# Softmax divided on GpSimd, in place on the probabilities, instead of on the gate

## The chip, the cores and the metric

The kernel runs on one core of a Trainium2 chip. The metric is the device time of one execution in microseconds (us). The core has five engines that run side by side, each through its own instructions in a fixed order: PE (TensorE, the matrix engine; its weight loads are listed apart as PEld), DVE (VectorE), ACT (ScalarE), POOL (GpSimd) and SP (SyncE, which here issues the DMA transfers). An instruction that needs another engine's result waits on a semaphore, and everything behind it on its own engine waits with it.

## The reference

One encoder layer is applied to two sequences of 2048 tokens with 1024 channels. After an RMS norm and one input projection, two attention branches run with 8 heads of 64 channels each: branch A attends inside a window of +-128 tokens and has 2 key heads and a learned sink, branch B attends to a neighbourhood of 8 x 16 on a grid of 64 columns with a learned bias. Each branch output is multiplied by SiLU of its gate, and output projections follow. What matters here:

```
# branch A, per block of 128 queries        # branch B, per grid row
m = max(max(sc), sink)                      pr = softmax(sc)
e = exp(sc - m)                             o  = pr @ v
denom = sum(e) + exp(sink - m)              o_b = o * silu(g_b)
pr = e / denom
o  = pr @ v
o_a = o * silu(g_a)
```

Division by the denominator is one factor per query and head, so it may be applied to the probabilities before the product with V, or to the gate that multiplies the product.

## The kernel before

The work is cut into 96 tiles of 128 tokens: `f` 0 to 31 is branch A (both sequences), 32 to 95 branch B in two halves of the heads. While tile `f` has its attention, PE fills the gaps with projection matmuls of later tiles (`stream`, made of `filler(f)`). Two tables, `PLAN_A` and `PLAN_B`, say at which share of a tile's projection work each piece of attention is emitted. PE's instructions are chained in exactly the order in which they are written (`pinned`); the instructions of ACT, DVE, POOL and SP are placed by a list scheduler that sees the dependencies.

An attention unit is four heads of one tile: branch A has two units for each `f` (`kv` 0 and 1), 64 in all, branch B one for each `f`, 64 in all. A unit goes through these steps:

- `sc(i)`, i = 0 to 3: two score matmuls for head i into a bank of PSUM; `softmax` then lets DVE add the mask or bias, write the scores to the SBUF tile `s` and take their row maximum.
- Behind `sc(3)`, `exps`: DVE negates the maxima (`nm`), ACT takes four exponentials in place on the four `s` tiles with their sums into `den`, branch A adds the sink, and DVE takes the reciprocal `rd`. DVE then multiplies `rd` by the token's norm factor `fct` (a column of `y` or `hr_b`), and POOL multiplies the 256 gate columns of the unit by it into a new tile `g2` (shown as `g` in the profile).
- `pt(j)`: PE transposes the probabilities into PSUM. In branch A, `pt(0)` transposes the first 128 columns of all four heads, `pt(1)` the next; in branch B, `pt(x)` transposes one head, in the order of heads 0, 2, 1, 3. ACT copies each result to SBUF as its high part and DVE makes the low part.
- `po`: PE multiplies the transposed probabilities with V.
- `fin` (in the next unit's time): PE transposes `g2`, and DVE multiplies it with the output.

A score row has 384 columns in branch A (256 at the ends of a sequence), and 288, 360, 384 or 512 in branch B. The gate `gs` of a tile lies in one of 6 buffers tagged `qg`, which also hold the queries.

The waits that matter are in these places: `pt` reads `s`, so it waits for whoever wrote `s` last; POOL also makes the low parts of the projections' inputs (L279), the rotary embedding of branch A (L405 to L408), the sum of two output halves in branch B (L694) and weight sums (L461).

Of the kernel before, what the change touches and what calls it, by code (L numbers as in the profile page):

```python
# [11 lines left out]
F32 = mybir.dt.float32  # L12
# [3 lines left out]
ALU = mybir.AluOpType  # L16
# [6 lines left out]
HD = 64  # L23
# [61 lines left out]
def emit(ctx, tc, io):  # L85
    nc = tc.nc
# [4 lines left out]
    def ptile(shape, tag, name):  # L91
        tag = PSM.get(tag, tag)
        return pp.tile(shape, F32, tag=tag, name=name, bufs=PSB[tag])
# [100 lines left out]
    def project(ps, xr, w, cost):  # L194

        for k in range(KT):
            for i, (a, b) in enumerate(((0, 0), (0, 1), (1, 0))):
                mm(ps, xr[:, a, k, :], w(k, b), k == 0 and i == 0, k == KT - 1 and i == 2)
                yield cost, k == KT - 1 and i == 2
# [11 lines left out]
    def exps(sm, n, fct, gs, sink=None):  # L211

        mx, nm, den, rd, ss = (sm[k] for k in ("mx", "nm", "den", "rd", "s"))
        if sink is None:
            nc.vector.tensor_scalar_mul(nm, mx, -1.0)  # L215
        else:
            nc.vector.scalar_tensor_tensor(out=nm, in0=mx, scalar=-1.0, in1=sink[1], op0=ALU.mult, op1=ALU.min)
        for i in range(4):
            nc.scalar.activation(ss[i][:, :n], ss[i][:, :n], AF.Exp, bias=nm[:, i:i + 1],  # L219
                                 accum_out=den[:, i:i + 1])  # L220
        if sink is not None:
            es = ap.tile([128, 4], F32, tag="es", name="es", bufs=3)
            nc.vector.tensor_tensor(out=es, in0=sink[0], in1=nm, op=ALU.add)
            nc.scalar.activation(es, es, AF.Exp)
            nc.vector.tensor_tensor(out=den, in0=den, in1=es, op=ALU.add)
        nc.vector.reciprocal(out=rd, in_=den)
        nc.vector.tensor_scalar_mul(rd, rd, fct)  # L227
        g2 = ap.tile([128, 4, HD], F32, tag="g2", name="g2", bufs=2)
        nc.gpsimd.tensor_tensor(out=g2, in0=gs.rearrange("p (h d) -> p h d", h=4),  # L229
                                in1=rd.unsqueeze(2).broadcast_to([128, 4, HD]), op=ALU.mult)  # L230
        return g2.rearrange("p h d -> p (h d)")

    def split_q(pqt, q1, q2):

# [10 lines left out]
    ap = ab_stack.enter_context(tc.tile_pool(name="ab", bufs=1))  # L245
# [98 lines left out]
    for i in range(4):  # L344
        nc.vector.tensor_tensor(out=tab[i // 2][:, i % 2], in0=cs[:, i % 2],
                                in1=rw[:, i].unsqueeze(1).broadcast_to([128, NT, 16]), op=ALU.mult)
# [29 lines left out]
    def proj_a(f):  # L376
        s, t = divmod(f, NT)
        xr, ms, (ssq, ee) = xt.pop(f), ms_a[:, f:f + 1], stats.pop(f)
        ka = 22 if f in last else KA
        pk = ptile([128, 256], "pj", "pk")  # L380
        yield from project(pk, xr, lambda k, b: wx[:, k, b, :], 112)
        sq2 = ap.tile([128, 512], F32, tag="sq", name="sq2", bufs=2)
        nc.scalar.activation(sq2[:, :128], pk[:, 0:128], AF.Square)
        nc.vector.tensor_reduce(out=ssq[:, 8:10], in_=sq2[:, :128].rearrange("p (h d) -> p h d", d=HD),
                                op=ALU.add, axis=AX.X)
        vr = ap.tile([128, 11], F32, tag="vr", name="vr", bufs=2)
        y = ap.tile([128, 12], F32, tag="y", name="y", bufs=4)
        nc.vector.tensor_scalar(out=vr[:, 8:10], in0=ssq[:, 8:10], scalar1=1.0 / HD, scalar2=ee,
                                op0=ALU.mult, op1=ALU.add)
        nc.vector.tensor_scalar(out=vr[:, 10:11], in0=ms, scalar1=EPS, scalar2=None, op0=ALU.add)  # L390
        rsqrt(ap, vr[:, 8:11], y[:, 8:11], 3, "rqk")
        nc.vector.tensor_scalar_mul(y[:, 11:12], y[:, 10:11], 0.5)
        kt = ap.tile([128, 4, HD], F32, tag="kt", name="kt", bufs=2)
        nc.vector.tensor_tensor(out=kt[:, 0:2, :], in0=pk[:, 0:128].rearrange("p (h d) -> p h d", d=HD),
                                in1=y[:, 8:10].unsqueeze(2).broadcast_to([128, 2, HD]), op=ALU.mult)
        pv = pk[:, 128:256].rearrange("p (h d) -> p h d", d=HD)
        nc.scalar.activation(vv[:, t, :, 0, :], pv, AF.Copy, scale=y[:, 10:11])
        nc.vector.scalar_tensor_tensor(out=vv[:, t, :, 1, :], in0=pv, scalar=y[:, 10:11],
                                       in1=vv[:, t, :, 0, :].bitcast(F32), op0=ALU.mult, op1=ALU.subtract)

        def rope(v, n, tb):
            r = ap.tile([128, 2, 8, 16], F32, tag="vr_", name="r", bufs=2)
            cb_ = tab[tb][:, 0, t, :].unsqueeze(1).broadcast_to([128, n, 16])
            sb_ = tab[tb][:, 1, t, :].unsqueeze(1).broadcast_to([128, n, 16])
            nc.gpsimd.tensor_tensor(out=r[:, 0, :n], in0=v[:, :, 0:16], in1=cb_, op=ALU.mult)  # L405
            nc.gpsimd.tensor_tensor(out=r[:, 1, :n, 0:8], in0=v[:, :, 8:16], in1=sb_[:, :, 0:8], op=ALU.mult)
            nc.gpsimd.tensor_tensor(out=r[:, 1, :n, 8:16], in0=v[:, :, 0:8], in1=sb_[:, :, 8:16], op=ALU.mult)
            nc.gpsimd.tensor_tensor(out=v[:, :, 0:16], in0=r[:, 0, :n], in1=r[:, 1, :n], op=ALU.add)  # L408
        rope(kt[:, 0:2, :], 2, 1)
        yield 0, False  # L410
        pq = ptile([128, 512], "pj", "pq")
        for i, c in enumerate(project(pq, xr, lambda k, b: w_q[k][:, b, :], 215)):
            if i in HQ and f > 0:
                HQ[i][0](f + 1, HQ[i][1])
            if i - 10 in HG and f in last:
                HG[i - 10][0](f + 1, HG[i - 10][1])
            yield c
            if i == ka:
                keys_a(kt, t)
        sq = ap.tile([128, 512], F32, tag="sq", name="sq", bufs=2)  # L420
        nc.scalar.activation(sq, pq, AF.Square)
        nc.vector.tensor_reduce(out=ssq[:, 0:8], in_=sq.rearrange("p (h d) -> p h d", d=HD), op=ALU.add, axis=AX.X)
        nc.vector.tensor_scalar(out=vr[:, 0:8], in0=ssq[:, 0:8], scalar1=1.0 / HD, scalar2=ee,
                                op0=ALU.mult, op1=ALU.add)
        rsqrt(ap, vr[:, 0:8], y[:, 0:8], 8, "rqa")
        q = ap.tile([128, 8, HD], F32, tag="qg", name="q", bufs=6)
        nc.vector.tensor_tensor(out=q, in0=pq.rearrange("p (h d) -> p h d", d=HD),
                                in1=y[:, 0:8].unsqueeze(2).broadcast_to([128, 8, HD]), op=ALU.mult)
        rope(q, 8, 0)
        yield 0, False  # L430
        pg = ptile([128, 512], "pj", "pg")
        for i, c in enumerate(project(pg, xr, lambda k, b: w_g[k][:, b, :], 215)):
            if i in HG and f > 0 and f not in last:
                HG[i][0](f + 1, HG[i][1])
            yield c
            if i + 24 == ka:
                keys_a(kt, t)
        gs = ap.tile([128, 512], F32, tag="qg", name="gs", bufs=6)
        nc.scalar.activation(gs, pg, AF.Tanh, scale=y[:, 11:12])
        nc.vector.scalar_tensor_tensor(out=gs, in0=gs, scalar=1.0, in1=pg, op0=ALU.add, op1=ALU.mult)  # L440
        held[f] = q, gs, y
        if t == NT - 1:
            regroup(s)
        if f == NT + 4:
            stats_b(0)
        yield 0, False
# [22 lines left out]
    def regroup(s):  # L469
        c = slice(NT * s, NT * s + NT)  # L470
        nc.sync.dma_start(ms_d[s * SEQ:(s + 1) * SEQ].rearrange("(t p) -> p t", p=128), ms_a[:, c])
        rows = ms_d.rearrange("(r k c) -> r k c", k=4, c=16)
        for i in range(NT * s, NT * s + NT):
            nc.sync.dma_start(ms_b[:, i:i + 1], rows[8 * (i // 4):8 * (i // 4) + 8, i % 4, :].rearrange("r c -> c r"))
# [84 lines left out]
    def proj_b(f):  # L559
# [11 lines left out]
        for i, c in enumerate(project(pk, xr, lambda k, b: w_qk[k][:, b, :], 215)):  # L571
            at = i + 24 if f in last else i
            if at in HX:
# [8 lines left out]
        nc.vector.tensor_scalar(out=vr, in0=ssq, scalar1=1.0 / HD, scalar2=ep_b[:, st:st + 1],  # L582
                                op0=ALU.mult, op1=ALU.add)
        rsqrt(ap, vr, y, 8, "rqb")
        qg = ap.tile([128, 2, 4, HD], F32, tag="qg", name="qg", bufs=6)
        kt = ap.tile([128, 4, HD], F32, tag="kt", name="kb", bufs=2)
        for dst, c in ((kt, 4), (qg[:, 0], 0)):
            nc.vector.tensor_tensor(out=dst, in0=pk[:, 64 * c:64 * c + 256].rearrange("p (h d) -> p h d", d=HD),
                                    in1=y[:, c:c + 4].unsqueeze(2).broadcast_to([128, 4, HD]), op=ALU.mult)
# [3 lines left out]
        for i, c in enumerate(project(pv, xr, lambda k, b: w_vg[k][:, b, :], 215)):  # L593
# [3 lines left out]
            if i == (KB if f not in last else 10):  # L597
                if f < 2 * NT + 2:
                    pending.append((kt, b, cb))
                else:  # L600
# [5 lines left out]
                                       in1=v[:, :, 0, :].bitcast(F32), op0=ALU.mult, op1=ALU.subtract)  # L606
# [5 lines left out]
        gs = qg[:, 1].rearrange("p h d -> p (h d)")  # L612
# [251 lines left out]
    with tc.tile_pool(name="c", bufs=1) as op:  # L864
# [179 lines left out]
        for m in range(7 * len(groups)):  # L1044
            n, i = divmod(m, 7)
# [104 lines left out]
```

## Time and profile before

| | before |
|---|---|
| median of 3 runs | 2651.11 us (2646.79 to 2652.35) |
| span of the profiled execution | 2651.7 us |
| the profiled execution's own time | given as its span alone; nothing is listed around it |
| granted TensorE clock over the span | 0.990 |
| PE busy | 2570.5 us, 97% |
| PE weight loads | 2270.6 us, 86% |
| DVE busy | 1952.0 us, 74% |
| ACT busy | 1500.2 us, 57% |
| POOL busy | 703.2 us, 27% |

The span lies within the three runs, 0.6 us over their median, so sums made against it hold for the runs too. Branch A's units run from about 60 to 830 us, branch B's from about 890 to 1940 us, and the rest is the output projection. A busy time of PE says that matmuls follow one another, not that each is as fast as it can be, so the idle time and the granted clock have to be read with it.

### The profile page before, as it was taken

Reading aid. Unit: us, or ns where it says so; the run is one execution under the profiler, and the core shown is the slowest. Engines: PE = TensorE matmul, PEld = TensorE weight load, DVE = VectorE, ACT = ScalarE, POOL = GpSimd, SP = SyncE. Lnnn points to the kernel's source line nnn. Section 1 sums busy time; section 2 is a strip of 40 time slices with the busy share of each in tenths; the row PEclk is TensorE's granted clock in tenths of the full one; section 3 lists DMA queues with packets and bytes.
Section 4 is the critical chain, followed back from the end, with each engine's and each line's share of the span. In section 5 each row is a group of like instructions: output and inputs, shape, how many; then the busy total and the mean of one; then the engine's idle time right before and its main releaser. Section 6 shows DMA issues by size and latency. Waiting matters only on the chain. (4 is left out here: it accounts for less than half of the span.)

```text
span 2651.7 us, 46657 instructions
## 1 busy us (share of the span) xinstructions
PE 2570.5 (97%) x16080; PEld 2270.6 (86%) x16080; DVE 1952.0 (74%) x5702; ACT 1500.2 (57%) x3519; POOL 703.2 (27%) x804
## 2 busy tenths in 40 slices
PE   7999999999989999999899999999989999999999
PEld 6888878888877888888788888888989999999999
DVE  6888878888887788788888888788665548555554
ACT  5776667676765566666676666666532214222322
POOL 3222222222222223223223222221123323223321
PEclk9999999999999999999999999999999999999999
DMA  6333322111233455555655554446675445223221
GB/s 208 101 100 102 108 74 77 58 55 52 55 98 117 150 170 171 181 177 160 221 167 165 185 170 153 148 152 205 184 235 195 158 158 194 79 97 107 80 76 48
DMA packets 230973, 357.48 MB, mean 135 GB/s; under 512 B 38321, under 2 KB 115761, under 8 KB 225585
## 3 DMA queue, kind: packets, MB, share of 16 engines
q1 hardware_dynamic: 230736, 354.51, 42.4%
q8 instruction: 127, 2.08, 0.3%
q14 instruction: 110, 0.89, 0.1%
HBM read 266.33 MB, written 105.92 MB: 140 GB/s over the span
## 5 line engine op out<-in xcount | busy, mean ns | idle before, releaser
L219 ACT ACTIVATE s<-s,nm 128x384 f32<-128x384 f32 (+4 forms) x512 | 306.3, 600 | 274.9 <-DVE nm L215 183.7
L189 PE MATMUL pvg<-wb,xr 128*128 128x512 f32 x1536 | 457.4, 405 | 0.0
L189 PE MATMUL pqk<-wa,xr 128*128 128x512 f32 x1536 | 436.6, 407 | 0.0
L279 POOL TENSOR_TENSOR xr<-stx,xr 128x512 fp32r<-128x512 f32 x192 | 246.9, 1296 | 396.1 <-ACT xr L278 369.2
L189 PEld LDWEIGHTS pqk<-wa,xr 128*128 128x128 f32 x1536 | 267.1, 189 | 36.8
L189 PEld LDWEIGHTS pvg<-wb,xr 128*128 128x128 f32 x1536 | 269.1, 190 | 31.8
L189 PE MATMUL pg<-wb,xr 128*128 128x512 f32 x768 | 231.9, 409 | 1.3 <-ACT wb L142 0.9
L189 PE MATMUL pq<-wa,xr 128*128 128x512 f32 x768 | 223.0, 404 | 3.5 <-DVE wa L143 2.3
L973 PE MATMUL acca<-opd,s 128*128 128x256 f32 x1344 | 169.6, 289 | 15.2 <-DVE r L992 13.6
L973 PEld LDWEIGHTS acca<-opd,s 128*128 128x128 f32 x1344 | 167.7, 197 | 15.8 <-DVE r L992 10.0
L189 PEld LDWEIGHTS pq<-wa,xr 128*128 128x128 f32 x768 | 141.6, 191 | 27.3 <-DVE wa L143 2.6
L204 DVE CUSTOM_DVE_ANT_0 s<-scb,bias 128x288 f32<-128x288 f32 (+3 forms) x256 | 141.9, 555 | 30.3 <-PE scb L189 26.4
L229 POOL TENSOR_TENSOR g<-qg,rd 128x256 f32<-128x256 f32 x64 | 39.2, 613 | 453.4 <-DVE rd L227 385.8
L668 DVE TENSOR_TENSOR p_t<-ptb,p_t 96x384 fp32r<-96x384 f32 (+3 forms) x256 | 149.6, 586 | 12.6 <-ACT p_t L667 9.1
L189 PEld LDWEIGHTS pob<-p_t,vw 128*128 128x128 f32 (+2 forms) x832 | 130.7, 190 | 32.4 <-ACT q1b L240 15.5
L189 PEld LDWEIGHTS pg<-wb,xr 128*128 128x128 f32 x768 | 137.2, 189 | 22.5 <-DVE wb L143 1.4
L667 ACT CAST p_t<-ptb 96x384 fp32r<-96x384 f32 (+3 forms) x256 | 129.8, 509 | 46.8 <-PE ptb L192 44.8
L556 DVE SCALAR_TENSOR_TENSOR ks_b<-pktb,wk,ks_b 64x128 fp32r<-64x128 f32 x256 | 115.2, 450 | 53.9 <-ACT ks_b L555 47.3
L189 PE MATMUL pob<-p_t,vw 128*128 128x256 f32 (+2 forms) x832 | 143.2, 285 | 5.4 <-ACT q1b L240 5.4
L189 PE MATMUL sc<-ks_a,q 128*128 128x384 f32 (+1 forms) x512 | 133.0, 351 | 13.2 <-DVE mx L204 6.4
L555 ACT ACTIVATE ks_b<-pktb,wk 64x128 fp32r<-64x128 f32 x256 | 124.9, 489 | 20.2 <-DVE ks_b L556 12.2
L204 DVE CUSTOM_DVE_ANT_0 s<-sc,mask 128x384 f32<-128x384 f32 (+1 forms) x256 | 136.0, 533 | 0.2
(197 smaller groups left out, 5826.3 us busy)
## 6 DMA issues: line engine op xcount, KB each, us to landing
stx<-x_b SPq DMA_DIRECT2D x128, 256.0 KB
vw<-v_d SPq DMA_DIRECT2D x112, 256.0 KB
stx<-x_a SPq DMA_DIRECT2D x64, 256.0 KB
stn<-x_n SPq DMA_DIRECT2D x64, 256.0 KB
v_d<-vb SPq DMA_DIRECT2D x64, 256.0 KB
x1r<-x_d SPq DMA_DIRECT2D x16, 1024.0 KB
y_t<-r SPq DMA_DIRECT2D x64, 256.0 KB
v_d<-vb SPq DMA_DIRECT2D x96, 128.0 KB
```

The lines of the kernel that those rows point to most:

```text
L189: pinned(nc.tensor.matmul(out, lhsT, rhs, start=start, stop=stop))
L204: nc.vector.tensor_tensor_reduce(out=s[:, :n], in0=ps[:, :n], in1=bias, scale=1.0, scalar=-3.0e38, op0=ALU.add, op1=ALU.max, accum_out=sm[ ...
L219: nc.scalar.activation(ss[i][:, :n], ss[i][:, :n], AF.Exp, bias=nm[:, i:i + 1], accum_out=den[:, i:i + 1])
L229: nc.gpsimd.tensor_tensor(out=g2, in0=gs.rearrange("p (h d) -> p h d", h=4), in1=rd.unsqueeze(2).broadcast_to([128, 4, HD]), op=ALU.mult)
L279: nc.gpsimd.tensor_tensor(out=lo, in0=raw, in1=hi.bitcast(F32), op=ALU.subtract)
L555: nc.scalar.activation(hi, pkt[a:a + 64, i], AF.Copy, scale=wk[a:a + 64, 1:2])
L556: nc.vector.scalar_tensor_tensor(out=lo, in0=pkt[a:a + 64, i], scalar=wk[a:a + 64, 1:2], in1=hi.bitcast(F32), op0=ALU.mult, op1=ALU.subtract)
L667: nc.scalar.copy(p_t[:kc, :nch, 0], pf)
L668: nc.vector.tensor_tensor(out=p_t[:kc, :nch, 1], in0=pf, in1=p_t[:kc, :nch, 0].bitcast(F32), op=ALU.subtract)
L973: pinned(nc.tensor.matmul(ps[:, kk], w[k][:, a, c:c + 128], o[:, b, k], start=i in (0, 1, 4) and kk == 0 and k == 0 and j == 0, stop=k == ...
```

## The change

The gate is left as it is. DVE's multiplication of `rd` by `fct` goes, and so does POOL's multiplication of the gate. Instead POOL multiplies each of the four `s` tiles, in place, by its head's column of `rd` and by `fct`: four instructions for a unit, each over all columns of the score row. The transposes of the gate in `fin` read `gs` directly. Since `gs` is now needed until `fin`, tag `qg` gets 7 buffers instead of 6; the two buffers of `g2` are gone.

```diff
@@ exps
         nc.vector.reciprocal(out=rd, in_=den)
-        nc.vector.tensor_scalar_mul(rd, rd, fct)
-        g2 = ap.tile([128, 4, HD], F32, tag="g2", name="g2", bufs=2)
-        nc.gpsimd.tensor_tensor(out=g2, in0=gs.rearrange("p (h d) -> p h d", h=4),
-                                in1=rd.unsqueeze(2).broadcast_to([128, 4, HD]), op=ALU.mult)
-        return g2.rearrange("p h d -> p (h d)")
+        for i in range(4):
+            nc.gpsimd.tensor_scalar(out=ss[i][:, :n], in0=ss[i][:, :n], scalar1=rd[:, i:i + 1], scalar2=fct,
+                                    op0=ALU.mult, op1=ALU.mult)
+        return gs
@@ proj_a (q and gs) and proj_b (qg)
-        q = ap.tile([128, 8, HD], F32, tag="qg", name="q", bufs=6)
+        q = ap.tile([128, 8, HD], F32, tag="qg", name="q", bufs=7)
...
```

In the listings below a row is a line of the kernel, an operation, what it writes and reads, and the tile's size; x4 is a run of four alike. Lines of the changed kernel are numbered one lower from L230 on.

POOL's order in branch A before, over one unit with `kv` 0 and one with `kv` 1:

```order
L405 TENSOR_TENSOR r<-kt,tab_203 128x32
L406 TENSOR_TENSOR r<-kt,tab_203 128x2x8
L407 TENSOR_TENSOR r<-kt,tab_203 128x2x8
L408 TENSOR_TENSOR kt<-r 128x2x16
L229 TENSOR_TENSOR g_3284<-gs,rd 128x256
L405 TENSOR_TENSOR r<-q,tab_202 128x128
L406 TENSOR_TENSOR r<-q,tab_202 128x8x8
L407 TENSOR_TENSOR r<-q,tab_202 128x8x8
L408 TENSOR_TENSOR q<-r 128x8x16
L229 TENSOR_TENSOR g_3439<-gs,rd 128x256
L279 TENSOR_TENSOR xr<-stx,xr 128x512 x2
```

The same place now:

```order
L404 TENSOR_TENSOR r<-kt,tab_203 128x32
L405 TENSOR_TENSOR r<-kt,tab_203 128x2x8
L406 TENSOR_TENSOR r<-kt,tab_203 128x2x8
L407 TENSOR_TENSOR kt<-r 128x2x16
L228 TENSOR_SCALAR s<-s,rd,y 128x384 x4
L404 TENSOR_TENSOR r<-q,tab_202 128x128
L405 TENSOR_TENSOR r<-q,tab_202 128x8x8
L406 TENSOR_TENSOR r<-q,tab_202 128x8x8
L407 TENSOR_TENSOR q<-r 128x8x16
L228 TENSOR_SCALAR s<-s,rd,y 128x384 x4
L278 TENSOR_TENSOR xr<-stx,xr 128x512 x2
```

The four instructions stand exactly where the one stood; nothing else on POOL changes its place in branch A.

PE's order is the same row by row, but for the gate's name in `fin`. One unit of branch A with `kv` 0, before; the three rows of `pt` are those that read `s`:

```order
L192 MATMUL pgt<-ident,g_3439 128x128 x2
L189 MATMUL pq<-wa_99,xr 128x512
L189 MATMUL pq<-wa_100,xr 128x512 x3
L189 MATMUL pq<-wa_101,xr 128x512 x3
L189 MATMUL pq<-wa_102,xr 128x512 x2
L192 MATMUL pt<-ident,s 128x128 x4
L189 MATMUL pq<-wa_102,xr 128x512
L192 MATMUL pt<-ident,s 128x128 x4
L189 MATMUL pg<-wb_103,xr 128x512 x3
L192 MATMUL pt<-ident,s 128x128 x4
L189 MATMUL pg<-wb_104,xr 128x512 x3
```

No projection matmul has been moved between the scores and the transposes.

ACT's order around the transposes of a unit with `kv` 1, before and then now (`pr` is the copy of a transpose's result, `xr` the high part of a later tile's input):

```order
L537 COPY ot<-po 64x256
L278 CAST xr<-stx 128x512
L240 CAST q_3473<-pqt 64x512
L237 CAST q_3474<-pqt 64x512
L517 CAST pr<-pt 128x512 x2
L240 CAST q_3474<-pqt 64x512
L517 CAST pr<-pt 128x512
L278 CAST xr<-stx 128x512
```

```order
L536 COPY ot<-po 64x256
L239 CAST q_3491<-pqt 64x512
L236 CAST q_3492<-pqt 64x512
L516 CAST pr<-pt 128x512
L277 CAST xr<-stx 128x512
L516 CAST pr<-pt 128x512
L239 CAST q_3492<-pqt 64x512
L516 CAST pr<-pt 128x512
L277 CAST xr<-stx 128x512
```

The first `xr` now stands behind the first copy of a transpose instead of ahead of it. DVE and SP have a few such swaps of neighbours; on DVE the multiplication of `rd` (L227) is gone.

More of the change, by code (lines that the diff above doesn't have):

```diff
@@ L437, in proj_a @@
                 keys_a(kt, t)
-        gs = ap.tile([128, 512], F32, tag="qg", name="gs", bufs=6)
+        gs = ap.tile([128, 512], F32, tag="qg", name="gs", bufs=7)
         nc.scalar.activation(gs, pg, AF.Tanh, scale=y[:, 11:12])
@@ L584, in proj_b @@
         rsqrt(ap, vr, y, 8, "rqb")
-        qg = ap.tile([128, 2, 4, HD], F32, tag="qg", name="qg", bufs=6)
+        qg = ap.tile([128, 2, 4, HD], F32, tag="qg", name="qg", bufs=7)
         kt = ap.tile([128, 4, HD], F32, tag="kt", name="kb", bufs=2)
```

## The prediction

> **What bounds the kernel now.** I read the page's busy times first, then the list of PE's waits, then the timeline of single units in branch A and branch B.
>
> ```profile
> span 2651.7 us, 46657 instructions
> PE 2570.5 (97%) x16080; PEld 2270.6 (86%) x16080; DVE 1952.0 (74%) x5702; ACT 1500.2 (57%) x3519; POOL 703.2 (27%) x804
> PE pt L192 <- ACT s L219: 6.3, 4, 5.3
> ```
>
> PE is idle for 2651.7 - 2570.5 = 81 us in all, and of the probabilities' transposes `pt` only four had to wait for the exponentials, 6.3 us together. No row of PE's waits names POOL. So PE sets the time, its order is fixed, and each microsecond that an instruction of PE waits is a microsecond of the end unless PE would have waited later anyway. The question is how close behind the softmax the transposes stand. A unit of branch A with `kv` 0, then one with `kv` 1 (start, length, engine, line, operation):
>
> ```profile
> 250.90 0.61 ACT L219 ACTIVATE s<-s,nm 128x384 f32<-128x384 f32 x1
> 251.50 0.19 ACT L224 ACTIVATE es<-es 128x4 f32<-128x4 f32 x1
> 251.99 0.18 DVE L226 RECIPROCAL rd<-den 128x4 f32<-128x4 f32 x1
> 252.46 0.21 DVE L227 TENSOR_SCALAR rd<-rd,y 128x4 f32<-128x4 f32 x1
> 252.60 0.58 PEld L192 LDWEIGHTS pt<-ident,s 128*128 128x128 f32 x4
> 252.75 0.61 POOL L229 TENSOR_TENSOR g<-gs,rd 128x256 f32<-128x256 f32 x1 [1.13 <-DVE rd L227]
> 252.83 0.60 PE L192 MATMUL pt<-ident,s 128*128 128x128 f32 x4
> ...
> 263.58 0.18 DVE L226 RECIPROCAL rd<-den 128x4 f32<-128x4 f32 x1
> 264.60 0.60 PE L192 MATMUL pt<-ident,s 128*128 128x128 f32 x4
> 265.75 1.29 POOL L279 TENSOR_TENSOR xr<-stx,xr 128x512 fp32r<-128x512 f32 x1 [0.76 <-ACT xr L278]
> L192 PE MATMUL pt<-ident,s x736: 270/272/477, 62.5 to 831.5; 128*128 128x128 f32 x184
> ```
>
> The last exponential ends at 251.51, `rd` at 252.17, and PE transposes at 252.83. Before, only the exponentials had to be ready, and the gate's factor had time until `fin` in the next unit. After the change four POOL instructions stand between 252.17 and the transposes, with 0.66 us of room here and 0.84 us in the second unit (263.76 to 264.60). In branch B a row of `pt` is one head (0, 2, 1, 3 in turn), so less has to be ready at once:
>
> ```profile
> 1054.35 0.18 DVE L226 RECIPROCAL rd<-den 128x4 f32<-128x4 f32 x1 [1.26 <-ACT s L219]
> 1054.86 0.60 PE L192 MATMUL ptb<-ident,s 128*128 128x128 f32 x4
> 1056.23 0.60 PE L192 MATMUL ptb<-ident,s 128*128 128x128 f32 x4
> ...
> 1086.37 0.18 DVE L226 RECIPROCAL rd<-den 128x4 f32<-128x4 f32 x1 [0.71 <-ACT s L219]
> 1087.74 0.49 PE L192 MATMUL ptb<-ident,s 128*96 128x128 f32 x3
> 1088.98 0.49 PE L192 MATMUL ptb<-ident,s 128*96 128x128 f32 x3
> ...
> 1102.70 0.18 DVE L226 RECIPROCAL rd<-den 128x4 f32<-128x4 f32 x1 [0.83 <-ACT s L219]
> 1103.67 0.49 PE L192 MATMUL ptb<-ident,s 128*128 128x128 f32 x3
> 1104.91 0.49 PE L192 MATMUL ptb<-ident,s 128*128 128x128 f32 x3
> ```
>
> These are rows of 512, 288 and 384 columns.
>
> **The price of one POOL multiplication.** No row of before has a POOL tensor_scalar on a tensor. The nearest, with mean ns ahead of the second bar:
>
> ```profile
> L279 POOL TENSOR_TENSOR xr<-stx,xr 128x512 fp32r<-128x512 f32 x192 | 246.9, 1296 | 396.1 <-ACT xr L278 369.2 <-PE ptb L192 12.0 <-DMA wb<-w_in_c 7.7
> L939 POOL TENSOR_TENSOR opd<-sum,opd 128x1024 fp32r<-128x1024 f32 x28 | 70.9, 2531 | 233.3 <-ACT opd L925 233.3
> L229 POOL TENSOR_TENSOR g<-gs,rd 128x256 f32<-128x256 f32 x64 | 39.2, 613 | 96.3 <-DVE rd L227 95.1 <-DVE rd L226 0.9 <-PE pt L192 0.3
> L354 POOL MEMSET q<- 64x512 f32 x2 | 1.0, 521 | 0.1
> masks.py:199 POOL TENSOR_SCALAR_AFFINE_SELECT ident<-ident 128x128 f32<-128x128 f32 x1 | 0.3, 292 | 0.1
> masks.py:197 POOL MEMSET ident<- 128x128 f32 x1 | 0.2, 205 | 0.3 <-POOLq L1142 0.3
> ```
>
> Upper bound: two tensors read. From 512 to 1024 columns, (2531 - 1296) / 512 = 2.41 ns a column and 62 ns fixed, so 988 ns for 384 columns. Lower bound: nothing read. From 128 to 512, (521 - 205) / 384 = 0.82 ns a column and 100 ns fixed, so 416 ns. The only row with one tensor read and one written, the affine select, took 292 ns at 128 columns, where the two lines give 370 and 205: the middle. I take the middle line, 80 + 1.62 ns a column: T = 0.70 us at 384, 0.50 at 256, 0.55 at 288, 0.66 at 360, 0.91 at 512.
>
> The Trainium skill (GPSIMD Engine Reference, sections 3.1 and 4.1) tells to keep elementwise work on VectorE, and gives about 1.8 cycles an element for a tight one-input loop, 769 ns measured at 512; in proportion that is an estimate of 577 ns at 384. By it the sum below would be some 45 us smaller. No run here shows that figure yet; the affine select's 292 ns is above its proportion, 192.
>
> **The change, part by part.**
>
> Branch A, 384 columns. POOL begins 0.08 us after DVE (252.67 to 252.75), and a weight load precedes its matmul by 0.23 (252.60 to 252.83). The fourth head is ready for its matmul at 252.17 + 0.08 + 4T + 0.23 = 252.48 + 4T; the fourth transpose of the first row starts at 252.83 + 0.60 - 0.27 = 253.16. PE is held for 4T - 0.68. With `kv` 1 it is 264.07 + 4T against 264.93, or 4T - 0.86. The mean, 4T - 0.77, is 2.04 us.
>
> ```profile
> L204 DVE CUSTOM_DVE_ANT_0 s<-sc,mask 128x384 f32<-128x384 f32 x224 | 122.8, 550 | 0.2
> L219 ACT ACTIVATE s<-s,nm 128x512 f32<-128x512 f32 x64 | 45.5, 712 | 27.4 <-DVE nm L215 27.1
> ```
>
> 224 rows of four heads are 56 units: 56 x 2.04 = 114 us. The other 8 units have 256 columns: 8 x (4 x 0.50 - 0.77) = 10 us.
>
> Branch B: 16 units of each width (64 rows of four heads for 512, the same for the others). At 512 the third multiplication, head 2, counts: 1054.53 + 0.31 + 3T = 1054.84 + 3T against 1056.23, 1.34 us; 16 x 1.34 = 21. At 384: 1103.19 + 3T against 1104.91, 0.39; 16 x 0.39 = 6. At 288 head 2 is ready at 1086.86 + 1.64 = 1088.50, ahead of 1088.98: nothing. For 360, between, I put 2. The sum of the waits is 114 + 10 + 21 + 6 + 2 = 153 us.
>
> What comes back: in branch A DVE runs behind PE at the end of the scores, and may catch up while PE is held:
>
> ```profile
> 258.07 0.51 PE L189 MATMUL sc<-ks_a,q 128*128 128x384 f32 x2
> 259.26 0.55 DVE L204 CUSTOM_DVE_ANT_0 s<-sc,mask 128x384 f32<-128x384 f32 x1
> ```
>
> It takes the last score row 0.68 us after PE ended it (258.58 to 259.26). That is the most that a unit could win, 56 x 0.68 = 38 us; the least is nothing, as all of DVE's work for this place comes from PE too. I take 0.2 us a unit, 11 us.
>
> The clock. PE's granted clock falls to half in stretches of 3.41 us. Four of them (busy PE, then the clock):
>
> ```profile
> 56.24:59.65 3.41, 1.58 (x8) 1.37 (x9) 3.09 (x18) 0.25 (x2) 1.26 (x1) 1.00 1.04 287
> 59.65:63.06 3.41, 3.41 (x19) 2.85 (x18) 2.20 (x14) 3.36 (x13) 1.04 (x5) 1.00 0.28 99
> 1838.00:1841.41 3.41, 1.52 (x11) 1.10 (x10) 3.12 (x10) 3.09 (x8) 0.61 (x1) 1.00 0.90 237
> 1841.41:1844.82 3.41, 2.50 (x11) 2.21 (x11) 3.22 (x9) 3.29 (x9) 0.00 (x0) 0.50 0.98 344
> ```
>
> A stretch with 1.83 us of idle PE left the next at full clock, one with 1.89 put it at half. So a wait of some 1.86 us in one stretch costs another 3.41 / 2 = 1.7 us. A wait of 2.04 us falls into one stretch far enough in (3.41 + 2.04 - 2 x 1.86) / 3.41 = 51% of positions; one of 1.84 us, after DVE's gain, never. With half of the 56 units on each side I take 14 drops, and 4 at places where PE waits already: 18 x 1.7 = 31 us.
>
> The Trainium skill (TensorE: Matmul & The Clock Gate, Part 1 and its summary) says that half rate comes after an idle window of about 3.4 us and advises against gaps over some 3 us. By that rule waits of 2 us would leave the clock alone, and the sum would lack the 31 us. The trace disagrees on how idle the window must be (1.89 us were enough) and agrees on its length.
>
> Costs nothing, and gains nothing: DVE's multiplication L227 (0.21 us in the row above) goes, but POOL starts from `rd` and the formulas already count from there. The gate's multiplication leaves POOL. `fin` reads a gate that is ready long before, and 7 buffers replace 6 so that its longer life holds up no query. Behind the four multiplications POOL's queue has the rotary embedding or `xr`: POOL would be done at 263.84 + 2.81 = 266.65, so the `xr` of 265.75 comes 0.9 us later, for a tile whose projection PE has not begun. ACT's swapped `xr` waits for PE's transposes now, by the same 2 us, with the same cover; if it went, a projection matmul of PE would be late next. POOL's busy time grows by 224 x 0.70 + 32 x 0.50 + 64 x (0.55 + 0.66 + 0.70 + 0.91) = 353, less 128 x 0.61 = 78, to about 980 us, still no bound.
>
> Sum: 153 - 11 + 31 = 173 us on a span of 2651.7: 2825 us. The span is 0.6 us above the runs' median, so the same number stands for the runs.
>
> **The rivals.**
>
> The clock falls in most units. It decides from T of about 0.75 us, where every unit of branch A waits over 2.2 us. With the two-tensor line: A 56 x (3.95 - 0.77) + 8 x (4 x 0.68 - 0.77) = 194, B 16 x (2.50 + 1.24 + 0.8) = 73, and drops in some 85% of 56 units and 10 of B, 58 x 1.7 = 98: 365 us, 3017 us. For it: every tensor row of POOL beside the select is on that line. Against: those read two tensors.
>
> POOL is far slower, as for an operation with two pointers to scalars and no row like it. From T = 1.1 us upward the time is over 3070 us.
>
> Not slower: POOL is fast enough that the four fit the room. It decides at 4T under 0.77, T under 0.19 us; then all waits are nothing and the time is 2652 us, or a little under it if DVE's lighter load spares some of the few us that PE waits for `s`. Against: the memset, which reads nothing, needs 521 ns for 512 columns.
>
> The change not doing what it says would be a scheduler that moved work between scores and transposes; PE's order shows none.
>
> The low end: with the memset line, T = 0.42, A gives 56 x 0.89 + 8 x 0.47 = 54, B 16 x 0.50 = 8 (at 512 the first head now counts, T - 0.02), no drops: 62, or 2714 us. DVE's gain could still come off, but the affine select at 292 ns is well over this line's 205, so I put the end at 2725.
>
> **How the numbers follow.** The forecast, 2725 to 2900 us, has a chance of 0.66; the clock's rival, 2900 to 3070, 0.24; the slow POOL, over 3070, 0.06; not slower, 0.04, half of it faster by over 0.2% and half within, which is about what a measurement of this kernel can tell from no change. The range is 2725 to 3000, with the forecast and over half of the first rival. Slower 0.96, same 0.02, faster 0.02.
>
> **What would show it.** POOL rows of `s<-s,rd` at 384 columns near 700 ns; PE waiting for POOL at `pt`, 120 to 200 us in about 64 waits or more, and at `ptb` some 30 us, mostly at 512 columns; branch A's stretch longer by about 130 us and branch B's by about 35; more stretches of half clock inside both branches; the output projection unchanged. A POOL duration off the middle line moves the sum by 56 x 4 = 224 us for each us of T in branch A alone, and would be the first thing to make the prediction wrong; a catch-up of DVE over 0.2 us is the second.

## The result, and the profile after

| | before | after |
|---|---|---|
| median of 4 runs | 2651.73 us (2646.79 to 2653.43) | 2805.97 us (2804.10 to 2807.72) |
| span of the profiled execution | 2651.7 us | 2802.3 us (its own time is 2804.1) |
| start to the first exponentials | 59.7 us | 59.5 us |
| branch A, first to 65th unit's exponentials | 827.3 us | 913.8 us |
| branch B, 65th to 128th unit's | 1044.1 us | 1105.9 us |
| the rest | 720.6 us | 723.1 us |

The changed kernel takes 1.0584 times the time of before, 95% interval 1.0568 to 1.0599. Branch A grew by 86.5 us, branch B by 61.8, all else by 2.3. From the page of the changed kernel, the engines' busy time:

```profile
span 2802.3 us, 47369 instructions
PE 2627.2 (94%) x16080; PEld 2274.3 (81%) x16080; DVE 1935.9 (69%) x5574; ACT 1500.0 (54%) x3519; POOL 955.0 (34%) x1188
```

Its longest waits of PE (in total, times, longest):

```profile
PE pt L192 <- POOL s L228: 68.0, 195, 6.1
PE ptb L192 <- POOL s L228: 32.6, 34, 4.6
PE ptb L192 <- DVE o_tb L696: 15.2, 39, 0.8
```

POOL, which no wait of PE named before, now holds it at the transposes. The third row is one that the prediction did not have. These rows count idle time between matmuls only; a transpose that runs alone, behind a wait for its weight load, delays PE by more than the wait that it shows, as the timeline of a branch A unit (`kv` 0) tells:

```profile
276.16 0.18 DVE L226 RECIPROCAL rd<-den 128x4 f32<-128x4 f32 x1
276.51 2.59 POOL L228 TENSOR_SCALAR s<-s,rd,y 128x384 f32<-128x384 f32 x4 [0.65 <-DVE rd L226]
277.23 0.33 PE L192 MATMUL pt<-ident,s 128*128 128x128 f32 x1
277.87 0.33 PE L192 MATMUL pt<-ident,s 128*128 128x128 f32 x1 [0.31 <-POOL s L228]
278.51 0.33 PE L192 MATMUL pt<-ident,s 128*128 128x128 f32 x1 [0.31 <-POOL s L228]
279.16 0.33 PE L192 MATMUL pt<-ident,s 128*128 128x128 f32 x1 [0.31 <-POOL s L228]
```

The four transposes, which followed one another in 0.60 us before, now start 0.64 us apart, at POOL's pace: each waits for its head. POOL's price by shape (mean ns ahead of the second bar):

```profile
L228 POOL TENSOR_SCALAR s<-s,rd,y 128x384 f32<-128x384 f32 x224 | 145.6, 664 | 66.4 <-DVE rd L226 60.8 <-ACT ot L536 5.7
L228 POOL TENSOR_SCALAR s<-s,rd,hr_b 128x512 f32<-128x512 f32 x64 | 49.4, 786 | 73.5 <-DVE rd L226 73.5
L228 POOL TENSOR_SCALAR s<-s,rd,hr_b 128x288 f32<-128x288 f32 x64 | 36.3, 582 | 123.0 <-DVE rd L226 96.8 <-PE pqtb L192 26.1
```

An instruction of 384 columns shows 0.66 us and follows the one ahead of it by 0.64. From 288 to 384 columns it grows by 0.85 ns a column, from 384 to 512 by 0.95.

### The profile page after: what moved, and what is told of

Same layout as the page of the kernel before. It is cut to its first block, busy times and chain, and to the rows that moved or that the text cites. A ratio compares the mean times of both kernels' runs of the same rounds, so it can differ in the third digit from the quotient of the medians.

```text
span 2802.3 us, 47369 instructions
## 1 busy us (share of the span) xinstructions
PE 2627.2 (94%) x16080; PEld 2274.3 (81%) x16080; DVE 1935.9 (69%) x5574; ACT 1500.0 (54%) x3519; POOL 955.0 (34%) x1188
## 5 line engine op out<-in xcount | busy, mean ns | idle before, releaser
L228 POOL TENSOR_SCALAR s<-s,rd,hr_b 128x288 f32<-128x288 f32 (+3 forms) x256 | 168.3, 672 | 451.2 <-DVE rd L226 425.1
L192 PE MATMUL pt<-ident,s 128*128 128x128 f32 x736 | 158.3, 297 | 68.5 <-POOL s L228 68.0
L192 PEld LDWEIGHTS pt<-ident,s 128*128 128x128 f32 x736 | 95.8, 143 | 130.8 <-POOL s L228 121.8
L517 DVE TENSOR_TENSOR pr<-pt,pr 128x512 fp32r<-128x512 f32 x184 | 126.5, 688 | 99.7 <-ACT pr L516 99.5
L228 POOL TENSOR_SCALAR s<-s,rd,y 128x384 f32<-128x384 f32 (+1 forms) x256 | 162.8, 650 | 77.7 <-DVE rd L226 71.2
L192 PE MATMUL ptb<-ident,s 128*128 128x128 f32 (+2 forms) x832 | 139.6, 282 | 48.2 <-POOL s L228 32.6
L192 PEld LDWEIGHTS ptb<-ident,s 128*128 128x128 f32 (+2 forms) x832 | 94.5, 138 | 105.3 <-POOL s L228 56.9
L516 ACT CAST pr<-pt 128x512 fp32r<-128x512 f32 x184 | 108.0, 588 | 108.0 <-PE pt L192 106.5
```

The costliest lines, as they stand in the source:

```text
L192: pinned(nc.tensor.transpose(out, in_, ident))
L228: nc.gpsimd.tensor_scalar(out=ss[i][:, :n], in0=ss[i][:, :n], scalar1=rd[:, i:i + 1], scalar2=fct, op0=ALU.mult, op1=ALU.mult)
L516: nc.scalar.copy(pr[:, 0], pf)
L517: nc.vector.tensor_tensor(out=pr[:, 1], in0=pf, in1=pr[:, 0].bitcast(F32), op=ALU.subtract)
```

## The experiments

**One branch at a time.** First branch A alone, then branch B alone:

```diff
+        if sink is None:        # a_only: branch B's gate as before   (b_only: if sink is not None)
+            nc.vector.tensor_scalar_mul(rd, rd, fct)
+            g2 = ...
+            return g2.rearrange("p h d -> p (h d)")
         for i in range(4):
             nc.gpsimd.tensor_scalar(...)
```

> Division on the probabilities by POOL in branch A alone, branch B's gate as before. My theory: the two stages add up, so this keeps the 86.5 us by which branch A's stretch grew (from first to 65th unit's exponentials) and drops the 61.8 us of branch B: about 2738 us, 1.033 of before. Rival: the growth in branch B is a late effect of branch A or of the seventh buffer: then branch B stays long and the time is near 2800 us.

> Division by POOL in branch B alone. My theory: 61.8 us of growth, about 2713 us, 1.023 of before, with PE waiting both for POOL's s and for DVE's o_tb. Rival as for a_only: near 2665 us if branch B's growth needs branch A's change.

Measured: 2732.85 us, ratio 1.0302 (1.0285 to 1.0319), and 2721.22 us, ratio 1.0255 (1.0238 to 1.0272). Branch B's stretch was 1036.2 us in the first, branch A's 827.1 in the second: each branch grows only where it is changed, and the ratios' excesses add to 5.6% against 5.8%. Both kernels have the seventh buffer, so that buffer alone costs nothing. The unchanged branch B of the first is even 7.9 us shorter than before; why, no run tells. The waits of PE in the second kernel show the same two rows for branch B:

```profile
PE ptb L192 <- POOL s L234: 33.7, 34, 4.6
PE ptb L192 <- DVE o_tb L702: 15.2, 39, 0.5
```

**The `o_tb` sum off POOL's queue.**

```diff
-            nc.gpsimd.tensor_tensor(out=o_t.rearrange("p i (r c) -> p i c r", c=16),
+            nc.vector.tensor_tensor(out=o_t.rearrange("p i (r c) -> p i c r", c=16),
```

> The changed kernel with the sum of the two output halves of branch B (o_tb, L693) on DVE instead of POOL, so that it no longer stands behind four multiplications. My theory: the o_tb sum was late on POOL's queue, and with it the PSUM bank of the gate's transposes, for which PE's second to fourth ptb row waited. Without it the units of 384, 360 and 288 columns lose about 0.67, 0.7 and 0.3 us each and those of 512 little: about 27 us less than the changed kernel, 2779 us, and no PE wait for o_tb in the profile. Rival: branch B's extra wait comes from the multiplications alone (head order); then the time stays at 2800 to 2810 us, or grows by DVE's added 64 x 0.4 us.

Measured: 2786.74 us, ratio 1.0503 (1.0485 to 1.0520), 19 us less than the changed kernel; branch B's stretch fell by 16.7 us to 1089.2, and the wait for `o_tb` is gone from PE's list. The changed kernel's timeline shows the chain that it removed, in a unit of 384 columns:

```profile
1217.63 0.18 DVE L226 RECIPROCAL rd<-den 128x4 f32<-128x4 f32 x1 [0.51 <-ACT s L219]
1217.99 2.58 POOL L228 TENSOR_SCALAR s<-s,rd,hr_b 128x384 f32<-128x384 f32 x4 [7.64 <-DVE rd L226]
1220.54 0.75 POOL L693 TENSOR_TENSOR o_tb<-otb 128x256 f32<-128x256 f32 x1
1221.32 0.42 DVE L696 TENSOR_TENSOR o_tb<-pgtb,o_tb 128x256 f32<-128x256 f32 x1 [1.95 <-POOL o_tb L693]
1221.89 0.52 PE L192 MATMUL ptb<-ident,s 128*128 128x128 f32 x3 [0.42 <-DVE o_tb L696]
```

POOL reaches the sum only after the four multiplications; DVE had been idle for 1.95 us waiting for it; DVE's product reads the last of the three PSUM banks that the gate's transposes share with `ptb`; and PE's third `ptb` row starts 0.15 us after that bank is free. The gain fell short of the 27 us. With the sum on DVE the timeline of the same place shows it during POOL's third multiplication, and POOL late:

```profile
1215.57 3.05 POOL L228 TENSOR_SCALAR s<-s,rd,hr_b 128x384 f32<-128x384 f32 x4 [7.13 <-DVE rd L226]
1216.96 0.59 DVE L693 TENSOR_TENSOR o_tb<-otb 128x256 f32<-128x256 f32 x1
```

Four took 3.05 us instead of 2.58 while DVE added two SBUF tensors. The Trainium skill (SBUF — State Buffer, "Who interferes with whom") says that a DVE instruction with two SBUF inputs contends with a GpSimd instruction that reads SBUF, and that the shared ports are an exclusive lock; the lost 0.47 us, most of the 0.59 that the DVE instruction took, fits that.

**DVE's removed multiplication alone.** The kernel before without L227; its gates lack the norm factor.

> The kernel before without DVE's multiplication of rd by fct (64 + 64 small instructions left out, so the gate lacks the norm factor). My theory: DVE is not what PE waits for there, 2651 us, ratio 1.000 within 0.002. Rival: DVE's lag in branch A shortens by 0.2 us a unit and PE gains some of it, 2640 us.

Measured: 2650.29 us, ratio 0.9988 (0.9978 to 0.9997). That is 3 us less than the kernel before by the medians, and 6 us at the far end of the interval: what the change took off DVE gains next to nothing.

**Later transposes.**

```diff
-    (0.75, 1, "pt", 0), (0.79, 1, "pt", 1), (0.88, 1, "pt", 2),
+    (0.93, 1, "pt", 0), (0.95, 1, "pt", 1), (0.98, 1, "pt", 2),
-    (0.45, 1, "pt", 0), (0.52, 1, "pt", 1), (0.60, 1, "pt", 2), (0.66, 1, "po", 0), (0.74, 1, "pt", 3), (0.80, 1, "po", 1),
+    (0.53, 1, "pt", 0), (0.60, 1, "pt", 1), (0.66, 1, "pt", 2), (0.72, 1, "po", 0), (0.80, 1, "pt", 3), (0.86, 1, "po", 1),
```

The second kernel has this table, the `o_tb` sum on DVE as above, and in branch B the heads in the order of their transposes:

```diff
-        for i in range(4):
+        for i in ((0, 1, 2, 3) if sink is not None else (0, 2, 1, 3)):
```

> The changed kernel with the transposes of the probabilities emitted later: branch A's three at 0.93, 0.95 and 0.98 of the unit's projection work instead of 0.75, 0.79 and 0.88, branch B's (with the products behind them) 0.06 to 0.08 later. My theory: what costs is only that PE reaches the transposes before POOL is done. Some 2 us of projection work more ahead of them in branch A and 1.2 us in branch B cover the 1.76 us and the 0.3 to 1.4 us by which PE was held: branch A's stretch back to about 830 us, branch B's to about 1070, 2670 to 2690 us. Rival: the later transposes run into the next unit's scores, which take the same three PSUM banks and come at 0.04 of the next unit; PE then waits for the copies out of them by ACT and DVE (0.6 and 0.7 us each), about 1 us a unit, and the time stays over 2730 us.

> As late_pt, and the o_tb sum of branch B on DVE, and branch B's four multiplications in the order in which its transposes read the heads (0, 2, 1, 3). My theory: every wait that the runs showed is covered, so the time comes to that of the kernel before within 0.5%, 2650 to 2665 us, and not under 2640, since PE is the bound in both. Rival as for late_pt: over 2720 us.

Measured: 2761.61 us, ratio 1.0409 (1.0393 to 1.0424), and 2738.84 us, ratio 1.0320 (1.0302 to 1.0339). Both expectations failed. Both times lie where the rivals put them, over 2730 and 2720 us, but their reason, the waits for the copies, is only part of it: half of POOL's wait at `pt` stayed, 36.3 us of 68.0. PE's waits in the first of the two:

```profile
PE pt L192 <- POOL s L228: 36.3, 98, 6.5
PE pob L189 <- DVE p_t L667: 15.8, 33, 1.1
PE sc L189 <- DVE pr L517: 14.0, 31, 1.9
```

A shift of 0.18 is taken from the unit's projection work alone, 13008 / 2 ns by the kernel's own table, so about 1.2 us and not the 2 us that I had counted, against a hold of 1.76. What it did cover came back in part as waits further on: the scores wait for the copies out of the banks, the products with V for the copies of the transposes. With the `o_tb` sum moved and the heads in the order in which they are read, branch B grew by 27.6 us (1071.7) and branch A, where neither applies, by 58.7 (886.0).

**The same division on DVE, and on both engines.**

```diff
-            nc.gpsimd.tensor_scalar(out=ss[i][:, :n], ...
+            nc.vector.tensor_scalar(out=ss[i][:, :n], ...                      # dve_div
+            eng = nc.gpsimd if i < 2 else nc.vector                            # split_div
+            eng.tensor_scalar(out=ss[i][:, :n], ...
```

> The changed kernel with the same four multiplications on DVE instead of POOL. My theory: the wait is 4T less the room whatever engine does it. DVE's CAST of 512 columns takes 0.42 us, so T is about 0.33 us for 384: 4T - 0.77 = 0.55 us a unit in branch A, 56 x 0.55 = 31 us, nothing in branch B but a later o_tb no more: about 2685 us. DVE gets 512 x 0.33 = 170 us more work (to 79% busy). Rival: DVE's load, not T, decides: DVE already runs 0.7 us behind PE at branch A's last score row, and its 1.3 us more per unit go straight into that lag: over 2740 us.

> The changed kernel with heads 0 and 1 divided on POOL and heads 2 and 3 on DVE, side by side. My theory: PE is held for as long as the longer of the two chains, less the room: in branch A 2 x 0.642 + 0.18 - 0.69 = 0.77 us instead of 1.76, so branch A's stretch grows by some 35 to 45 us instead of 86; branch B's by less than 50, as only two multiplications stand ahead of the o_tb sum: 2725 to 2745 us. Rival: DVE's 0.95 us more per unit delay its own copies and the next unit's scores, as they did with all four on DVE (branch B grew by 84 us there): 2760 us or more.

Measured: 2786.09 us, ratio 1.0498 (1.0482 to 1.0513), and 2762.09 us, ratio 1.0409 (1.0392 to 1.0427): both times the rival's number, the second by only 2 us, and its reason only in part. On DVE one multiplication of 384 columns took 0.472 us, not 0.33. DVE's lag at branch A's last score row, which the rival named, did not grow (0.5 and 0.7 us at the median for `kv` 0 and 1), and branch A grew by 51 us, less than with POOL; branch B grew by 84 us, more than with POOL. PE waits there for DVE's multiplications and for DVE's other work. The group of the multiplications in the kernel on DVE:

```profile
L228 DVE TENSOR_SCALAR s<-s,rd,y 128x384 f32<-128x384 f32 x224 | 93.0, 472 | 0.1
```

Two of its waits of PE at branch B's tiles:

```profile
PE ptb L192 <- DVE s L228: 24.1, 17, 4.0
PE pktb L192 <- DVE otb L686: 22.2, 34, 0.9
```

Side by side the two engines get in each other's way. A unit of branch A with two heads on each:

```profile
266.06 0.18 DVE L226 RECIPROCAL rd<-den 128x4 f32<-128x4 f32 x1
266.41 2.05 POOL L229 TENSOR_SCALAR s<-s,rd,y 128x384 f32<-128x384 f32 x2 [0.66 <-DVE rd L226]
266.59 0.85 DVE L229 TENSOR_SCALAR s<-s,rd,y 128x384 f32<-128x384 f32 x2
```

POOL's two took 2.05 us instead of 1.30; the 0.75 us more are nearly DVE's 0.85. So half of the work on POOL saved 0.5 us of the chain, not 1.3, and branch A still grew by 55 us, branch B by 57. PE's longest wait there is again for POOL at `pt`, 58.3 us, and not for DVE as the rival had it.

**Twice the chain.**

```diff
             nc.gpsimd.tensor_scalar(out=ss[i][:, :n], in0=ss[i][:, :n], scalar1=rd[:, i:i + 1], scalar2=fct, ...)
+            nc.gpsimd.tensor_scalar(out=ss[i][:, :n], in0=ss[i][:, :n], scalar1=1.0, scalar2=1.0, ...)
```

> The changed kernel with a second POOL multiplication (by 1.0) behind each of the four, so that T doubles to 1.28 us for 384 columns. My theory: PE is held for 8 x 0.642 + 0.10 - 0.77 = 4.5 us a unit in branch A, so branch A's stretch grows by 56 x 4.5 + 8 x 3.6 - 24 = 257 us instead of 86; branch B's by 16 x (3.2 + 2.2 + 2.1 + 1.4) = 142 us or more with the late o_tb. And now each wait is well over 1.86 us, so that the clock falls to half in nearly every unit of branch A and half of branch B's: 90 drops x 1.7 = 150 us. Together about 3200 us. Rival: no clock drops at such short repeated waits: about 3050 us and a granted clock near 0.98.

Measured: 3076.84 us, ratio 1.1595 (1.1572 to 1.1619). Branch A's stretch is 1088.9 us, 262 over before, branch B's 1200.9, 157 over. The time lies between the two expectations. The second pass took 0.516 us at 384 columns, so the part of the sum without the clock, which had both passes at 0.642, was too high. The clock did fall. Branch A's stretch in the changed kernel (start and end, length, PE busy, granted clock, DMA share, GB/s):

```profile
59.50:973.30 913.80, 837.08 (x4364) 0.98 0.26 76
```

And in the kernel with the doubled chain:

```profile
59.70:1148.60 1088.90, 909.07 (x4365) 0.91 0.21 64
```

A mean of 0.91 is a loss of up to 0.09 x 1088.9 = 98 us, if PE set the pace all through, against 0.02 x 913.8 = 18.

**The price of the scalars.** Two kernels with `rd` multiplied on DVE again:

```diff
+        nc.vector.tensor_scalar_mul(rd, rd, fct)
         for i in range(4):
-            nc.gpsimd.tensor_scalar(..., scalar1=rd[:, i:i + 1], scalar2=fct, op0=ALU.mult, op1=ALU.mult)
+            nc.gpsimd.tensor_scalar(..., scalar1=rd[:, i:i + 1], scalar2=None, op0=ALU.mult)                  # one_ptr
+            nc.gpsimd.tensor_scalar(..., scalar1=rd[:, i:i + 1], scalar2=1.0, op0=ALU.mult, op1=ALU.mult)     # one_ptr_x1
```

> The changed kernel with rd multiplied by fct on DVE first, as before the change, so that POOL's multiplication reads one scalar from memory instead of two. The multiplication by constants in two_pass took 0.516 us at 384 columns where the one with two scalars from memory took 0.664. My theory: each scalar costs half of the difference, 0.07 us, so T is 0.59; four of them save 0.30 us, and DVE's instruction ahead costs 0.25 to 0.45: the time stays within 10 us of the changed kernel's 2803. Rival: the price is per instruction with any scalar, T stays 0.66 and branch A alone grows by 64 x 0.3 = 19 us.

> As one_ptr (rd multiplied by fct on DVE first), but POOL's instruction has a second operation again, a multiplication by the constant 1.0. My theory: what made one_ptr's multiplication take 1.245 us at 384 columns is the missing second operation (2.5 ns a column instead of 0.83), not the number of scalars read from memory; with it, T is 0.59 (between 0.664 with two scalars from memory and 0.516 with none) and the time within 15 us of the changed kernel's 2803. Rival: an instruction with one scalar from memory is slow whatever its second operation, and the time stays near 3260 us.

Measured: 3261.55 us, ratio 1.2294 (1.2268 to 1.2320), against both theories, and 2861.64 us, ratio 1.0785 (1.0766 to 1.0804). The price in the first:

```profile
L229 POOL TENSOR_SCALAR s<-s,rd 128x384 f32<-128x384 f32 x288 | 353.5, 1245 | 247.4 <-ACT otb L686 143.6 <-DVE rd L227 70.5 <-PE pg L189 13.8
```

And in the second:

```profile
L229 POOL TENSOR_SCALAR s<-s,rd 128x384 f32<-128x384 f32 x288 | 163.6, 587 | 247.7 <-ACT otb L686 144.2 <-DVE rd L227 73.6 <-PE pg L189 13.1
```

The instruction with one operation takes twice as long as the same with a multiplication by 1.0 behind it. The theory of the second kernel holds for the instruction (587 ns against 0.59 us expected) but not for the time, which is 56 us over the changed kernel, 57 of it in branch A. Counted from the reciprocal `rd`, POOL is done only 0.25 us later in units with `kv` 0. But `rd` itself is late there: the scheduler has placed the square of a later tile's input (`stn`) ahead of the exponentials on ACT, and that square waits for its DMA:

```profile
195.27 0.16 DVE L217 SCALAR_TENSOR_TENSOR nm<-mx,snk 128x4 f32<-128x4 f32 x1
196.56 0.63 ACT L292 ACTIVATE stn<-stn 128x512 f32<-128x512 f32 x1 [2.69 <-DMA stn<-x_n]
197.19 0.60 ACT L219 ACTIVATE s<-s,nm 128x384 f32<-128x384 f32 x1
```

In units with `kv` 0 the first exponential starts 1.60 us after `nm` is ready at the median, in the changed kernel 0.03, and the 28 units of 384 columns are held for 103 us in all instead of 54. So by the trace most of the 57 us goes with this order, which the edit brought with it, and not with POOL's price; no run has the order alone. The kernel with one operation has the same order on ACT (1.56 us), so its 3261 us are not the price alone either. Some of the longer holds is lost clock. Two neighbouring stretches of the second kernel, the first with a wait in such a unit (busy PE, PEld, DVE, ACT and POOL, then the granted clock):

```profile
200.91:204.33 3.42, 1.77 (x10) 1.14 (x10) 0.99 (x4) 0.79 (x2) 2.26 (x4) 1.00 0.59 212
204.33:207.74 3.41, 3.41 (x12) 2.82 (x11) 2.33 (x5) 1.73 (x4) 0.00 (x0) 0.50 0.00 0
```

1.65 us of idle sufficed here. Branch A's granted clock is 0.96 instead of 0.98, at most 0.02 x 971 = 19 us.

## Why the prediction was right

The direction, the place and the sum held: 2806 us measured, 2825 predicted, with transposes that wait for POOL. The terms fit less well than their sum. Term by term, with the holds read as the growth from the scores' end to the unit's last transpose:

- **POOL's price.** Predicted 0.70 us at 384 columns, measured 0.642 to the next one; at 512, 0.91 against 0.748. It is not the middle line: 0.85 ns a column is near the memset's slope of 0.82, on a fixed part of some 0.32 us. At 384 the two cross near the middle, so the choice was lucky in its reason and good in its value; at 512 it was 20% high. The Trainium skill's figure, estimated at 577 ns, lies 10% under the measurement. With it the prediction would have lost more than the 45 us that it names: the holds fall under 1.86 us, so by its own rule for the clock the 14 drops, 24 us, would go too.
- **Branch A's holds.** Predicted 2.04 us a unit, 124 us for 64; measured 1.84 and 1.68 us at the median for `kv` 0 and 1, 111 us in all. The formula with the measured 0.642 and POOL's start 0.18 us after `rd` instead of 0.08 gives 4 x 0.642 + 0.10 - 0.77 = 1.90.
- **What came back.** Predicted 11 us, measured 24 as the difference of the holds and the stretch. The mechanism was another one: DVE's lag at the last score row did not shrink, but PE's scores ran closer together. Before, some of their weight loads waited for DVE's copies of the last transposes; held transposes give DVE that time. The waits of PE's weight loads for these copies, before and after:

```profile
PEld sc L189 <- DVE pr L518: 28.4, 62, 0.6
PEld sc L189 <- DVE pr L517: 1.6, 4, 0.7
```

Four score pairs of a `kv` 0 unit on the timeline of before:

```profile
268.38 0.61 PE L189 MATMUL sc<-ks_a,q 128*128 128x384 f32 x2
269.30 0.51 PE L189 MATMUL sc<-ks_a,q 128*128 128x384 f32 x2
269.97 0.62 PE L189 MATMUL sc<-ks_a,q 128*128 128x384 f32 x2 [0.17 <-DVE pr L518]
270.73 0.62 PE L189 MATMUL sc<-ks_a,q 128*128 128x384 f32 x2
```

The same on the timeline of after:

```profile
295.87 0.51 PE L189 MATMUL sc<-ks_a,q 128*128 128x384 f32 x2
296.69 0.86 PE L189 MATMUL sc<-ks_a,q 128*128 128x384 f32 x4
297.61 0.51 PE L189 MATMUL sc<-ks_a,q 128*128 128x384 f32 x2
```

They took 268.38 to 271.35, 2.97 us, before and 295.87 to 298.12, 2.25 us, after. At the median the `kv` 0 units gained 0.72 us.

- **Branch B.** Predicted 29 us, measured 65 in holds: 1.40 us a unit at 512 columns (1.34 predicted), but 0.96 at 384 (0.39), 1.09 at 360 (0.13) and 0.43 at 288 (nothing). The step that failed is the list of what stands behind the multiplications on POOL's queue: it named branch A's rotary embedding and `xr`, and left out branch B's `o_tb` sum, to which a PSUM bank is tied. The kernel with that sum on DVE showed it: holds of 0.19, 0.49 and 0.25 us at 384, 360 and 288, 1.27 at 512.
- **The clock.** Predicted 31 us, but both branches' mean clock moved by at most 0.01. The step that failed is the count of drops, half of the units, which stood on a hold of 1.84 to 2.04 us that was idle PE all through. The measured hold was 1.7 to 1.8, and less than half of it was idle, as the four transposes run one by one inside it. Branch A's stretch before, to be read with the one of the changed kernel above:

```profile
59.70:887.00 827.30, 801.18 (x4361) 0.99 0.28 84
```

Idle PE grew from 26 to 77 us, so by 51 / 64 = 0.8 us a unit; the other 36 us of the growth are matmuls that count as busy for longer. With the doubled chain it was 180 us, 2.4 a unit more than before, and the clock fell. The Trainium skill (TensorE: Matmul & The Clock Gate, Part 1) asks for an idle window of about 3.4 us; 1.65 us of idle in one were enough in the run above, so the runs do not agree with it.

The sum: branch A 111 - 24 = 87, branch B 65 - 3 = 62, the rest 2, together 151 us on the span. The prediction had 113, 29 and 31 for the clock: 26 us too much in branch A and some 30 for the clock, against 33 too little in branch B. That errors of opposite sign left the sum only 22 us off was luck; the direction and the place were not. Its signs for the two stretches, about 130 and 35 us longer, were off in the same way. The rival of the clock needed T, the time of one multiplication, over 0.75 us and showed itself only where the chain was longer, doubled or with the slow instruction. The slow POOL came in one form, the instruction with a single operation. Not slower would have needed T under 0.19 us.

## What to carry to other kernels

A factor that may be applied in two places costs by its slack, not by its work: on the gate it had until the next unit, on the probabilities 0.7 us. That POOL, with its 252 us of added work, is still idle for two thirds of the span was no help. Price such a move as a chain against the room in front of the waiting engine, and then follow the moved engine's own queue to every instruction behind it that frees a buffer or a PSUM bank. And read the order of the other engines in every variant: a small edit let the scheduler put a wait for a DMA ahead of the exponentials, and the time then told more of that than of the price that it was to show.

## What the runs showed of the hardware

- POOL's tensor_scalar with one operation took 1.245 us at 384 columns and 1.577 at 512 (2.6 ns a column); with a second, idle multiplication 0.587 and 0.706 (0.93 ns a column). A multiplication by 1.0 made it twice as fast.
- Scalars read from memory cost POOL: 0.516 us with none, 0.587 with one, 0.664 with two at 384 columns.
- POOL and DVE multiplying in SBUF at the same time did not run side by side: POOL lost about as much as DVE took (0.75 of 0.85 us).
- Half clock followed a stretch of 3.41 us with only 1.65 us of idle PE in one kernel, while 1.83 us left the next stretch at full clock in the kernel before: the edge is not one number.
